# Gated DeltaNet chunk inverse: the last 64x64 merge level spread over both column halves of the TensorE array, with its evictions in two parts

## The chip, the cores and the metric

The kernel runs on one core of one Trainium2 chip. The metric is the device time of the whole launch in microseconds (us), as the median over runs of the same program. The profile is one profiled execution of the same program; its times are counted from the first instruction.

## The reference

One inference step of a two-layer decoder: layer 0 is a gated DeltaNet mixer, layer 1 an RWKV-7 mixer, each behind an RMSNorm and with a residual add. It runs on 1040 prompt tokens and on 8 x 8 sample tokens, 1104 columns in all, in fp32. What concerns the change is the chunk-wise delta rule of layer 0, which solves a unit lower triangular system for every chunk of 64 tokens and every head:

```python
L = jnp.where(strict, jnp.einsum('nbhik,nbhjk->nbhij', kb, k) * decay, 0.0)
A = L + jnp.eye(chunk, dtype=L.dtype)
rhs = jnp.concatenate([vb, kb * jnp.exp(gc)[..., None]], -1)
sol = lax.linalg.triangular_solve(A, rhs, left_side=True, lower=True, unit_diagonal=True)
u, wk = sol[..., :DV], sol[..., DV:]
...
v_new = u_c - jnp.einsum('bhck,bhkv->bhcv', w_c, S)
o = jnp.einsum('bhck,bhkv->bhcv', qd_c, S) + jnp.einsum('bhij,bhjv->bhiv', a_c, v_new)
S = S * jnp.exp(gl_c)[..., None, None] + jnp.einsum('bhck,bhcv->bhkv', kd_c, v_new)
```

There are 16 value heads and 8 key heads of width 128.

## The kernel before

Tokens are the columns of all activations, in three segments of 384, 384 and 336 columns (`SEGS`). Layer 0 loops over 8 key heads `j`; each carries two value heads. The kernel works with blocks of 128 tokens, so one segment of one key head has 6 systems (3 blocks x 2 value heads), and one key head has 18. The inverse of each 128x128 system is built in levels.

1. `gdn_prep` forms the scaled lower triangles `E` (kept as `G.LT`, one tile of 6 systems per segment) and sends their 32x32 diagonal blocks by DMA to a tile `invA` with one block per partition.
2. `inverse32` inverts these blocks on VectorE (31 steps of two instructions, L452 and L454).
3. The results come back by DMA into two tiles: `TT` (the transposed inverse, `TTs[...]`, one per segment) and `T1n`.
4. A first merge level joins 32x32 blocks to 64x64 ones. For each segment it forms Y (six systems, two halves, 32x32 matmuls into a PSUM bank of tag "r", evicted by VectorE at L668) and then U (evicted with a sign change by ScalarE through the helper at L62 into `TT`, and by VectorE at L679 into `T1n`).
5. A second merge level joins the 64x64 blocks to 128x128. This is the level that is changed. For each of the three segments there are six matmuls for Y: weights are rows 0 to 63 of `LT`, the moving data are rows 0 to 63 of `T1n`, and the output is partitions 64 to 127 of an "r" bank. One VectorE copy of 64x384 elements (L684) brings them into `Ys`, which lies in the tile that held `invA`. Then follow, for each segment, six matmuls for U: rows 64 to 127 of `Ys` and of `TT`, with the output on partitions 0 to 63 of an "r" bank, and one ScalarE activation of 64x384 elements (helper line L62, scale -1) into `TT`.

Where a matmul's operands start in the partitions sets the rows of the 128x128 array that it uses, and where its output starts sets the columns: all Y matmuls of this level use rows 0 to 63 and columns 64 to 127, all U matmuls rows 64 to 127 and columns 0 to 63.

After the inverse, `gdn_recur` steps through the 9 blocks of the head. In each step the state S is multiplied by the keys (`rA<-S,K`), VectorE forms X (L765), TensorE multiplies by `TT` (`rA<-X,TT`), ScalarE scales to w, TensorE forms the outputs and the state update, and VectorE updates S (L779). Its matmuls go to "r" banks as well; there are three of these.

All matmuls pass through the helper `mm` (L76), transposes through L73. The profile records each fp32 matmul as two passes, each with a weight load (PEld) and a matmul (PE).

The order of instructions on each engine is chosen by the framework's scheduler over layer 0 and the first part of layer 1, from the dependencies and its own timing model. It mixes the dense projections (`conv_tile` and `gdn_gate`: tiles dq, dk, dv, dz) of one head with the inverse and the recurrence of another. The last part, the RWKV wave, has its TensorE order written out by hand.

Of the kernel before, what the change touches and what calls it, by code (L numbers as in the profile page):

```python
# [10 lines left out]
AF = mybir.ActivationFunctionType  # L11
# [24 lines left out]
class Builder:  # L36
# [564 lines left out]
    def gdn_prep(self, j, G):  # L601
        nc, t, gp, fp = self.nc, self.t, self.gp, self.fp
# [7 lines left out]
        for s in range(3):  # L610
            q3 = slice(3 * s, 3 * s + 3)
            p = self.ps("f", 2, "sc")
# [37 lines left out]
        T1 = self.T1n  # L650
# [9 lines left out]
        v = lambda p, k: p[:, 0:6 * k].rearrange("p (c i) -> p c i", i=k)  # L660
        Y = [buf[:, 384 * s:384 * s + 384].rearrange("p (c i) -> p c i", i=64) for s in range(3)]
        for s, (LT, Ys) in enumerate(zip(G.LT, Y)):
            p = self.ps("r", 3, "Y")
# [5 lines left out]
        for s, (TT, Ys) in enumerate(zip(G.TT, Y)):  # L669
            p = self.ps("r", 3, "U")  # L670
# [8 lines left out]
            nc.vector.tensor_scalar(T1[32:64, 6 * s:6 * s + 6, 0:32], v(p, 32)[32:64], -1.0, None, op0=ALU.mult)  # L679
        for s, (LT, Ys) in enumerate(zip(G.LT, Y)):  # L680
            p = self.ps("r", 3, "Y")
            for c in range(6):
                self.mm(v(p, 64)[64:128, c], LT[0:64, c, 64:128], T1[0:64, 6 * s + c])
            nc.vector.tensor_copy(Ys[64:128], v(p, 64)[64:128])  # L684
        for s, (TT, Ys) in enumerate(zip(G.TT, Y)):
            p = self.ps("r", 3, "U")
            for c in range(6):
                self.mm(v(p, 64)[0:64, c], Ys[64:128, c], TT[64:128, c, 64:128])
            self.act(TT[0:64, :, 64:128], v(p, 64)[0:64], AF.Identity, scale=-1.0)

    def gdn_values(self, j, G, xh, xl):

# [1222 lines left out]
```

## Time and profile before

| | |
|---|---|
| median of 3 runs | 2376.5 us (2376.37 to 2380.79) |
| profiled execution, first to last instruction | 2369.3 us; no other time is given for it |
| TensorE matmul busy | 2188.7 us, 92% |
| TensorE weight load busy | 1982.0 us, 84% |
| VectorE busy | 1612.1 us, 68% |
| ScalarE busy | 1283.7 us, 54% |
| GpSimd busy | 1097.0 us, 46% |
| 64x64 matmul passes of this level, Y and U | 288 in 21.0 us and 288 in 19.5 us busy |
| Y evictions, 64x384 on VectorE | 24 in 13.2 us |
| U evictions, 64x384 on ScalarE | 24 in 11.1 us |

A busy time is the union of the instructions' durations on one engine, so passes that overlap count once; the mean of one instruction stands beside it in the groups' rows. Matmuls are pipelined, and the step from one start to the next is shorter than the duration of one.

### The profile page before, as it was taken

The numbers are of one execution on the slowest core, as the hardware profiler recorded it, in microseconds if no ns is written. First come the engines' busy times: TensorE is split into PE (matmuls) and PEld (weight loads), VectorE is DVE, ScalarE is ACT, GpSimd is POOL, SyncE is SP. The second block draws the span as 40 slices with busy tenths as digits, with TensorE's granted clock in tenths as the row PEclk, the third lists the DMA queues.
The fourth block names the chain that finished last, engine by engine and source line by source line (L and its number), as shares of the span: only waits on it lengthen the run. The fifth ranks groups of instructions, "written<-read, shape, count | busy, mean of one in ns | idle before, by whom it ended". The sixth has DMA issues, their size and how long they took to land. (4 is left out here: it accounts for less than half of the span.)

```text
span 2369.3 us, 54804 instructions
## 1 busy us (share of the span) xinstructions
PE 2188.7 (92%) x19737; PEld 1982.0 (84%) x19737; DVE 1612.1 (68%) x4201; ACT 1283.7 (54%) x3665; POOL 1097.0 (46%) x1542
## 2 busy tenths in 40 slices
PE   6989999999999999999999999998899899999896
PEld 5888989889898989898989998987778777778785
DVE  6878677685858686774346824479786567778754
ACT  5455645555656555466343746556454455667662
POOL 3435333443435343434232623444344667778764
PEclk9999999999999999999999999999999889999998
DMA  3323332323233333335162245566754544565543
GB/s 113 104 75 107 87 100 76 96 74 102 80 100 91 84 107 88 108 95 179 50 169 83 59 164 171 148 156 178 190 129 135 175 113 138 159 187 182 178 145 121
DMA packets 470922, 290.04 MB, mean 122 GB/s; under 512 B 188505, under 2 KB 456026, under 8 KB 470650
## 3 DMA queue, kind: packets, MB, share of 16 engines
q1 hardware_dynamic: 470650, 286.53, 42.8%
q8 instruction: 156, 2.56, 0.5%
q14 instruction: 116, 0.95, 0.1%
HBM read 200.53 MB, written 85.89 MB: 121 GB/s over the span
## 5 line engine op out<-in xcount | busy, mean ns | idle before, releaser
L90 POOL TENSOR_TENSOR wlo<-wraw,whi 128x512 fp32r<-128x512 f32 (+2 forms) x252 | 331.6, 1319 | 345.2 <-ACT whi L86 321.4
L76 PE MATMUL d<-xc,whi 128*128 128x384 f32 (+2 forms) x910 | 259.1, 341 | 5.3 <-POOL xc L90 2.5
L86 ACT CAST whi<-wraw 128x512 fp32r<-128x512 f32 (+2 forms) x252 | 151.5, 603 | 134.0 <-PE dq L76 50.4
L419 DVE SCALAR_TENSOR_TENSOR cvy<-raw,cw,cvy 128x408 f32<-128x408 f32 (+2 forms) x288 | 178.9, 634 | 17.0 <-ACT cvy L62 15.1
L76 PEld LDWEIGHTS d<-xc,whi 128*128 128x128 f32 (+1 forms) x910 | 167.6, 191 | 12.1 <-issue 3.4
L452 DVE TENSOR_TENSOR invtmp<-invA,invT 72x31 f32<-72x31 f32 (+31 forms) x403 | 165.5, 411 | 12.8 <-DMA invA<-ltd 4.4
L454 DVE TENSOR_TENSOR invT<-invT,invtmp 72x31 f32<-72x31 f32 (+31 forms) x403 | 165.5, 411 | 6.6
L76 PE MATMUL dz<-xc,whi 128*128 128x384 f32 (+1 forms) x480 | 149.6, 343 | 0.0
L76 PE MATMUL dv<-xc,whi 128*128 128x384 f32 (+1 forms) x480 | 146.8, 335 | 0.0
L76 PE MATMUL d<-xc,wlo 128*128 128x384 f32 (+2 forms) x428 | 142.4, 342 | 1.9 <-POOL wlo L90 1.9
L76 PE MATMUL d<-xa,whi 128*128 128x384 f32 (+3 forms) x450 | 139.7, 345 | 3.5 <-DVE xa L90 1.7
L868 POOL TENSOR_SCALAR Sb<-Sb,eglb 128x128 f32<-128x128 f32 x128 | 82.4, 662 | 87.8 <-DMA Sb<-in_state_gdn 62.3
L1506 POOL TENSOR_SCALAR y<-y,mv,grs 128x64 f32<-128x64 f32 x144 | 83.5, 600 | 41.3 <-DVE grs L106 39.6
L76 PE MATMUL dz<-xa,whi 128*128 128x384 f32 (+1 forms) x288 | 100.5, 349 | 0.0
L76 PE MATMUL dv<-xa,whi 128*128 128x384 f32 (+1 forms) x288 | 99.9, 347 | 0.1
L76 PEld LDWEIGHTS d<-xa,whi 128*128 128x128 f32 (+1 forms) x450 | 83.3, 190 | 11.0 <-issue 3.3
L76 PEld LDWEIGHTS dz<-xc,whi 128*128 128x128 f32 x480 | 89.9, 193 | 0.8
L76 PEld LDWEIGHTS dv<-xc,whi 128*128 128x128 f32 x480 | 88.6, 188 | 0.5 <-issue 0.4
L62 ACT ACTIVATE o<-rA,gcol 128x128 f32<-128x128 f32 x128 | 46.7, 372 | 72.4 <-DVE S L779 72.0
L76 PE MATMUL d<-xa,wlo 128*128 128x384 f32 (+3 forms) x252 | 85.9, 341 | 0.0
L76 PE MATMUL d<-xh,wlo 128*128 128x384 f32 (+1 forms) x256 | 83.8, 343 | 1.7 <-POOL wlo L90 1.7
L76 PEld LDWEIGHTS d<-xc,wlo 128*128 128x128 f32 (+1 forms) x428 | 81.1, 191 | 4.5 <-POOL wlo L90 2.2
(508 smaller groups left out, 7216.4 us busy)
## 6 DMA issues: line engine op xcount, KB each, us to landing
wraw<-in_gdn_w_in SPq DMA_DIRECT2D x96, 256.0 KB
wraw<-in_rwkv_w_rkvz SPq DMA_DIRECT2D x80, 256.0 KB
Sb<-in_state_gdn SPq DMA_DIRECT2D x64, 256.0 KB
wraw<-in_rwkv_w_o SPq DMA_DIRECT2D x40, 256.0 KB
E<-drow SPq DMA_DIRECT2D x24, 384.0 KB
attn<-drow SPq DMA_DIRECT2D x24, 384.0 KB
wraw<-in_gdn_w_out SPq DMA_DIRECT2D x36, 256.0 KB
out_s_gdn<-Sb SPq DMA_DIRECT2D x32, 256.0 KB
```

What stands on the lines that cost most here:

```text
L62: return self.nc.scalar.activation(out, in_, func, bias=bias, scale=scale, **kw)
L76: self.nc.tensor.matmul(out, lhsT, rhs, start=start, stop=stop)
L86: nc.scalar.copy(hi, x)
L90: e.tensor_tensor(lo, x, hi.bitcast(F32), op=ALU.subtract)
L419: nc.vector.scalar_tensor_tensor(y[:, 0:wd], raw[:, k:k + wd], cw[k], y[:, 0:wd], op0=ALU.mult, op1=ALU.add)
L452: nc.vector.tensor_tensor(tmp, A[:, j, j + 1:32].unsqueeze(2).broadcast_to([nb, n, m]), Tv[:, j, 0:m].unsqueeze(1).broadcast_to([nb, n, m] ...
L454: nc.vector.tensor_tensor(Tv[:, j + 1:32, 0:m], Tv[:, j + 1:32, 0:m], tmp, op=ALU.subtract)
L868: nc.gpsimd.tensor_scalar(Sb[:, u], Sb[:, u], self.eglb[:, hv, 4 * g + u:4 * g + u + 1], None, op0=ALU.mult)
L1506: nc.gpsimd.tensor_scalar(y6[:, q], y6[:, q], mv[:, q, 0:1], rs[:, q:q + 1], op0=ALU.subtract, op1=ALU.mult)
```

## The change

The six systems of a segment are dealt out to the two column halves: for Y, even systems stay in columns 64 to 127 and odd ones go to columns 0 to 63; for U the other way round. The rows of the array remain the same for both. In PSUM the six 64x64 results now lie in three 64-column slots on both partition halves, instead of six slots on one half. Each eviction is divided into two, one for each partition half: 64x192 elements each, written to every second system of the destination. Nothing else is edited; the number of matmuls is the same.

```diff
         for s, (LT, Ys) in enumerate(zip(G.LT, Y)):
             p = self.ps("r", 3, "Y")
+            w = p[:, 0:192].rearrange("p (c i) -> p c i", i=64)
             for c in range(6):
-                self.mm(v(p, 64)[64:128, c], LT[0:64, c, 64:128], T1[0:64, 6 * s + c])
-            nc.vector.tensor_copy(Ys[64:128], v(p, 64)[64:128])
+                a = 0 if c % 2 else 64
+                self.mm(w[a:a + 64, c // 2], LT[0:64, c, 64:128], T1[0:64, 6 * s + c])
+            for a, x in ((64, 0), (0, 1)):
+                nc.vector.tensor_copy(Ys[64:128, x::2], w[a:a + 64])
         for s, (TT, Ys) in enumerate(zip(G.TT, Y)):
             p = self.ps("r", 3, "U")
+            w = p[:, 0:192].rearrange("p (c i) -> p c i", i=64)
             for c in range(6):
-                self.mm(v(p, 64)[0:64, c], Ys[64:128, c], TT[64:128, c, 64:128])
-            self.act(TT[0:64, :, 64:128], v(p, 64)[0:64], AF.Identity, scale=-1.0)
+                a = 64 if c % 2 else 0
+                self.mm(w[a:a + 64, c // 2], Ys[64:128, c], TT[64:128, c, 64:128])
+            for a, x in ((0, 0), (64, 1)):
+                self.act(TT[0:64, x::2, 64:128], w[a:a + 64], AF.Identity, scale=-1.0)
```

## The prediction

> **What bounds the kernel now.** I read the page's busy shares and 40 slices first, then the windows of about one head each, then who waits for whom on TensorE, and last the matmuls of the edited step in order of time.
>
> ```profile
> span 2369.3 us, 54804 instructions
> ...
> PE 2188.7 (92%) x19737; PEld 1982.0 (84%) x19737; DVE 1612.1 (68%) x4201; ACT 1283.7 (54%) x3665; POOL 1097.0 (46%) x1542
> ...
> PE   6989999999999999999999999998899899999896
> ```
>
> TensorE is the full engine nearly everywhere. The windows sharpen this for the DeltaNet heads, which take about 130 us each (columns: stretch, length, then busy time of PE, PEld, DVE, ACT, POOL):
>
> ```profile
> core 0: us, PE busy (x) PEld busy (x) DVE busy (x) ACT busy (x) POOL busy (x), PEclk, DMA share, GB/s
> ...
> 230.00:360.00 130.00, 125.06 (x1025) 114.59 (x1026) 95.86 (x281) 71.93 (x231) 52.92 (x85) 0.98 0.33 89
> 360.00:490.00 130.00, 125.68 (x1030) 115.07 (x1029) 95.28 (x281) 72.56 (x231) 53.99 (x82) 0.98 0.34 92
> 490.00:620.00 130.00, 123.98 (x1017) 113.43 (x1018) 92.96 (x276) 71.12 (x229) 51.65 (x80) 0.99 0.33 90
> 620.00:750.00 130.00, 125.76 (x1044) 115.11 (x1043) 97.73 (x291) 74.17 (x238) 55.83 (x87) 1.00 0.35 94
> 750.00:880.00 130.00, 124.92 (x1025) 114.11 (x1025) 94.88 (x279) 71.75 (x230) 52.56 (x81) 0.99 0.32 89
> 880.00:1010.00 130.00, 126.56 (x1040) 116.55 (x1040) 95.85 (x288) 73.98 (x236) 55.94 (x85) 0.99 0.35 95
> ```
>
> PE is busy 125.3 of 130 us on average (96%), VectorE about 95, ScalarE about 73, and the granted clock is 0.98 to 1.00. So in these heads TensorE time is the time of the kernel, and the other two engines have 35 and 57 us of slack per head. What idles TensorE in the heads (window 140 to 1180 us) is small, and it is the recurrence, not the inverse:
>
> ```profile
> PE rA L76 <- DVE S L779: 8.7, 15, 2.1
> PE fhist L73 <- DVE lasts L437: 8.2, 7, 1.7
> PE rA L76 <- DVE X L765: 4.7, 7, 1.2
> ```
>
> **The change on TensorE.** The edited step is 48 groups of six 64x64 matmuls (8 heads, three segments, Y and U). Each fp32 matmul is recorded as two passes, so a group is 12 passes; all twelve sit in one quarter of the array now. The timeline of head 0 shows groups standing alone, two together and three together:
>
> ```profile
> 160.20 0.91 PE L76 MATMUL rY<-T1n,E 64*64 64x64 f32 x12
> ...
> 161.41 1.61 PE L76 MATMUL rY<-T1n,E 64*64 64x64 f32 x24
> ...
> 166.78 2.31 PE L76 MATMUL rU<-TT,invA 64*64 64x64 f32 x36
> ```
>
> Twelve more passes take 0.70 us more each time, so a pass follows the last one after 58 ns. One pass lasts 221 ns (rows below), so a lone group takes 0.91 - 0.22 = 0.69 us from its first start to its last: ten gaps of 58 ns and a first one of 0.11.
>
> After the change a group's even and odd matmuls alternate between the two column halves, over the same 64 rows. What matters is whether two column tiles that share their rows run side by side. Two places of this trace do that already. The state read (fsr) streams through four 32-column tiles on all 128 rows; and in the 32x32 level of this inverse the products marked invA,TT share rows 32 to 63 with half of those marked TT,invA, in the neighbouring 32 columns:
>
> ```profile
> 114.75 1.28 PE L76 MATMUL fsr<-Sb,kqm 128*32 128x128 f32 x34
> ...
> 155.97 0.19 PE L76 MATMUL rU<-invA,TT 32*32 32x32 f32 x1
> 155.98 0.21 PE L76 MATMUL rU<-TT,invA 32*32 32x32 f32 x2
> 156.00 0.19 PE L76 MATMUL rU<-invA,TT 32*32 32x32 f32 x1
> ...
> 172.27 0.38 PE L76 MATMUL rA<-X,TT 128*128 128x128 f32 x2
> ```
>
> ```profile
> L76 PE MATMUL rA<-X,TT 128*128 128x128 f32 x288 | 57.7, 287 | 4.8 <-DVE X L765 4.7
> L76 PE MATMUL fsr<-Sb,kqm 128*32 128x128 f32 x512 | 28.0, 280 | 0.9 <-POOL kqm L840 0.6
> L76 PE MATMUL rY<-T1n,E 64*64 64x64 f32 x288 | 21.0, 221 | 0.0
> L76 PE MATMUL rU<-TT,invA 64*64 64x64 f32 x288 | 19.5, 220 | 0.1
> ```
>
> Two rA passes over the full array are 0.38 - 0.29 = 0.09 us apart. The fsr passes stream the same 128 columns, yet 33 starts fit into 1.28 - 0.28 = 1.00 us: 30 ns each, about a third. In the 32x32 level a whole round of three tiles takes 0.03 us. So shared rows do not serialise.
>
> The Trainium skill, TensorE: Matmul & The Clock Gate, section Part 3 (Packing small matmuls), says that a weight load overlaps matmuls in flight only where the row group differs; here the row group is the same, and by that rule the change would gain nothing. The fsr rows speak against it, and I keep it as a rival.
>
> New group: each half has six passes, 0.11 + 4 x 0.058 = 0.34 us from first start to last, and the second half starts about 0.01 us after the first, so 0.35 instead of 0.69. Where groups stand together, 0.70 per group becomes 0.35. Saving 0.34 x 48 = 16.3 us. Something of this exists already: where a U follows a Y without a gap, as in four of the eight heads (the first is shown), the last three Y passes run beside U passes:
>
> ```profile
> 283.14 0.73 PE L76 MATMUL rY<-T1n,E 64*64 64x64 f32 x9
> 283.66 0.27 PE L76 MATMUL rU<-TT,invA 64*64 64x64 f32 x1
> 283.71 0.22 PE L76 MATMUL rY<-T1n,E 64*64 64x64 f32 x1
> 283.76 0.22 PE L76 MATMUL rU<-TT,invA 64*64 64x64 f32 x1
> ...
> 283.88 1.39 PE L76 MATMUL rU<-TT,invA 64*64 64x64 f32 x21
> ```
>
> That is 3 x 0.055 us in four heads, 0.7 us that is not saved a second time: 15.6 us. The halves alternate one by one in all 48 groups of the changed kernel's instruction order, so the scheduler does not undo it. I let 96% (the heads' busy share) reach the end: 15.0 us.
>
> **The change on the evictions.** Each group's one eviction becomes two of half the columns, 24 more on VectorE (Y, L684) and 24 more on ScalarE (U, through L62). No row is 64x192; these are around it:
>
> ```profile
> L668 DVE COPY invA<-rY 32x192 f32<-32x192 f32 x48 | 17.1, 357 | 6.8 <-PE rY L76 5.9
> L684 DVE COPY invA<-rY 64x384 f32<-64x384 f32 x24 | 13.2, 560 | 7.7 <-PE rY L76 7.3
> L784 DVE COPY o<-rA 64x128 f32<-64x128 f32 x16 | 4.7, 295 | 0.2
> L62 ACT ACTIVATE TT<-rU 32x192 f32<-32x192 f32 x48 | 15.4, 321 | 23.5 <-PE rU L76 22.9
> L62 ACT ACTIVATE TT<-rU 64x384 f32<-64x384 f32 x24 | 11.1, 477 | 1.2 <-PE rU L76 1.2
> L62 ACT ACTIVATE UV<-rA 64x128 f32<-64x128 f32 x144 | 35.8, 273 | 50.6 <-PE rA L80 50.3
> L76 PEld LDWEIGHTS rU<-TT,invA 64*64 64x64 f32 x288 | 17.7, 135 | 1.4 <-issue 1.1 <-DVE invA L684 0.2
> ```
>
> The same 192 elements per partition cost 357 ns on VectorE and 321 ns on ScalarE; the 64x128 rows (295 and 273) bound it below, the undivided evictions (560 and 477) above. I take 357 and 321: 2 x 357 - 560 = 154 ns more per Y and 2 x 321 - 477 = 165 ns more per U, hence 0.46 + 0.50 = 0.96 us per head, 7.7 us over the kernel if nothing hid it. What hides it is the dense projection work that stands between Y and U on TensorE: the last row shows 0.2 us in total for which a U waited on a Y copy. In the new order 4 of 8 heads keep 10 or more matmuls between the last Y and the first U and one keeps 7; the other three have none or two, but there the first Y stands well before the last, or the later U groups stand 10 or more matmuls on. I charge 1.0 us for two or three half-microsecond waits where this cover is thin; the ends are 0 and 7.7. The second copy waits only for the odd half, which ends with the even one, so the queue behind it (conv taps and the recurrence's X and S on VectorE) is late by 0.15 us, no more. The three "r" banks come free as much later. No DMA is added or moved by the text of the change.
>
> **The schedule.** The scheduler places instructions anew: the two TensorE orders agree up to head 0's merge and over the last 3,636 matmuls (the hand-ordered wave), and differ by local swaps between. That has no sign that I can derive. Its size I estimate from the six like windows: their busy times scatter by 0.88 us (standard deviation), so a redraw of some 12 windows (148 to 1,810 us) moves the sum by 0.88 x sqrt(12) x sqrt(2) = 4.3 us, or 5.5 us 8 times in 10.
>
> **Sum.** 15.0 - 1.0 = 14.0 us. The page gives the profiled execution as its span, 2369.3 us, and no other time; the median of the runs is 2376.5, 7.2 more. So the span should become 2355 and the time 2376.5 - 14.0 = 2362.5, with 2357 to 2368 as this case's own range.
>
> **Rivals.**
> *The evictions come onto the path* (0.15). U waits for the second Y copy and the recurrence for the second U eviction, in every head: all 7.7 us are paid, 15.0 - 7.7 = 7.3 remains, 2369. For it: the chain Y, copy, U, eviction is serial, and three heads have little between Y and U. Against it: the 0.2 us row, and VectorE's 35 us of slack. The Trainium skill, TensorEngine Tiling (Array Packing), section PSUM Bottleneck, warns of just this, that eviction may take over once tiling speeds up the matmuls.
> *The recurrence's waits grow* (0.13), the case on the slower side. Removing TensorE work and swapping neighbours leaves less filler between a head's S, X and w steps. The price is the 8.7 us in 15 waits, 0.58 each. It cancels the 14.0 at 24 more such waits and is slower by 0.2% (4.8 us) from 33, four per head; then about 2381. Typical of this case is 20 to 30 more, 2374 to 2380. Against it: only 15 such waits stand in 1040 us, and the work removed is 2 us in 130.
> *Shared rows serialise* (0.06), so that the change does not do what it says. If the halves simply take turns, nothing is saved and 1.0 is paid: 2377. If every change of half waits as a first pass does, 0.11 us a gap, a group takes 11 x 0.11 = 1.2 us instead of 0.69, 0.5 x 48 = 24 us more: 2401. The fsr rows are against both. The skill's row-group rule, above, belongs here.
>
> **How the numbers follow.** The forecast has 0.66. The range 2355 to 2374 takes the forecast with its schedule scatter, the eviction case and the lower edge of the waits case. A measurement can tell about 0.2%, 4.8 us: faster is below 2371.7, the same is up to 2381.3. Faster: 0.64 of the forecast, 0.12 of the evictions, 0.01 of the waits: 0.77. Slower: 0.05 of the waits, 0.03 of the serialising rows and 0.02 for schedule scatter on top: 0.10. The same: 0.13.
>
> **What would show it.** In the new profile, a lone group of twelve 64x64 passes at 0.57 us instead of 0.91, and the busy time of the rY and rU 64x64 matmuls down from 21.0 and 19.5 us to about 13 and 12; evictions of 64x192 near 357 and 321 ns, 48 of each; waits of rU on the L684 copies (then L687) below 2 us in total. The forecast is wrong if the twelve still take 0.9 us, if TensorE's waits on S, X and w grow by more than 5 us, or if a stretch after 1180 us, where nothing was edited, grows by several.

## The result and the profile after

The changed kernel takes 2390.7 us (median of 9 runs, 2380.6 to 2401.1) against 2375.4 for the one before on the same chip: a ratio of 1.0065, 95% interval 1.0046 to 1.0084. Forecast were 2362.5 us and a gain of 14.0; it became about 15 us slower, outside the range. Ratios and intervals, here and below, leave out the one slow run of all, 2407.5 us in experiment e8. The profiled execution spans 2386.5 us, 17.2 more than before's. The lines of its page that answer to those shown of before, with the granted TensorE clock by slices (PEclk, in tenths of full speed):

```profile
span 2386.5 us, 54833 instructions
...
PE 2186.4 (92%) x19737; PEld 1978.4 (83%) x19737; DVE 1627.2 (68%) x4225; ACT 1294.1 (54%) x3689; POOL 1101.1 (46%) x1542
...
PE   6989999999999999999999999988989888899995
...
PEclk9999999999999999999999999999999899999998
```

The groups of the edited step, from the views by form of TensorE, VectorE and ScalarE (busy time and mean, then idle time before them):

```profile
L76 PE MATMUL rU<-TT,invA 64*64 64x64 f32 x288 | 13.9, 250 | 0.5 <-PE rU L76 0.4
L76 PE MATMUL rY<-T1n,E 64*64 64x64 f32 x288 | 13.7, 243 | 4.7 <-DVE T1n L679 4.6
...
L687 DVE COPY invA<-rY 64x192 f32<-64x192 f32 x48 | 17.1, 356 | 5.4 <-PE rY L76 4.5
...
L62 ACT ACTIVATE TT<-rU 64x192 f32<-64x192 f32 x48 | 15.6, 325 | 2.9 <-PE rU L76 2.3
```

The edited matmuls fell from 21.0 + 19.5 = 40.5 us busy to 27.6, with means of 243 and 250 ns that a lower clock in some of them has lengthened; the divided evictions take 356 and 325 ns. The evictions are as forecast, the matmuls nearly so (about 25 us was forecast; see e9). But TensorE's whole busy time fell by 2.3 us only, and its waits in the window from 140 to 1180 us have another make-up than before:

```profile
PE fhist L73 <- DVE lasts L437: 10.0, 7, 2.0
PE rA L76 <- DVE S L785: 6.3, 12, 1.4
PE rA L76 <- ACT w L62: 4.9, 4, 2.8
PE rY L76 <- DMA T1n<-g_t: 4.9, 3, 3.9
PE rY L76 <- DVE T1n L679: 4.6, 5, 2.2
PE dk L76 <- DVE zg L726: 4.1, 3, 1.7
```

Two rows of before that the prediction does not show:

```profile
PE rY L76 <- DMA T1n<-g_t: 3.9, 1, 3.9
PE rA L76 <- ACT w L62: 3.2, 6, 0.9
```

Not there before are Y's waits on VectorE's T1n (4.6 us, up to 2.2) and those of the projection dk on `zg`, the output gate (4.1). The first is clear in head 2. ScalarE and VectorE in the timeline, with TensorE's passes:

```profile
421.76 0.56 PE L76 MATMUL rY<-T1n,E 64*64 64x64 f32 x12 [2.20 <-DVE T1n L679]
422.83 0.90 PE L76 MATMUL rY<-T1n,E 64*64 64x64 f32 x12 [0.51 <-DVE T1n L679]
...
420.25 0.49 ACT L62 ACTIVATE zg<-dz 128x384 f32<-128x384 f32 x1 [4.41 <-DMA ogd<-zg]
420.64 1.31 ACT L62 ACTIVATE TT<-rU 32x192 f32<-32x192 f32 x4
...
420.77 0.55 DVE L726 SCALAR_TENSOR_TENSOR zg<-zg,dz 128x384 f32<-128x384 f32 x1 [4.55 <-ACT zg L62]
421.36 0.35 DVE L679 TENSOR_SCALAR T1n<-rU 32x192 f32<-32x192 f32 x1
```

The scheduler has put `zg<-dz` ahead of the TT evictions of the first merge level on ScalarE, and ScalarE stands idle 4.41 us for a transfer. VectorE's product of zg waits 4.55 us for that, T1n is queued behind the product, and TensorE stands still for 2.20 and 0.51 us. The first lone group of this head takes 0.56 us. The second of the two waiting groups takes 0.90 us again, because the clock has just fallen (columns: stretch, length, busy times, then PEclk, DMA share, GB/s):

```profile
416.00:422.00 6.00, 3.80 (x68) 3.20 (x62) 1.39 (x4) 1.68 (x6) 0.00 (x0) 1.00 0.28 73
422.00:433.00 11.00, 10.49 (x83) 9.12 (x80) 4.26 (x10) 6.52 (x20) 5.82 (x9) 0.53 0.56 172
```

From 422.6 to 432.9 us TensorE is granted half its clock (0.5; called half clock from here on). The same stands behind the merges of heads 1 and 3 in this execution, 10.2 us each.

### The profile page after: what moved, and what is told of

It is laid out like the page before. It is cut to its first block, busy times and chain, and to the rows that moved or that the text cites. A ratio compares the mean times of both kernels' runs of the same rounds, so it can differ in the third digit from the quotient of the medians.

```text
span 2386.5 us, 54833 instructions
## 1 busy us (share of the span) xinstructions
PE 2186.4 (92%) x19737; PEld 1978.4 (83%) x19737; DVE 1627.2 (68%) x4225; ACT 1294.1 (54%) x3689; POOL 1101.1 (46%) x1542
## 5 line engine op out<-in xcount | busy, mean ns | idle before, releaser
L419 DVE SCALAR_TENSOR_TENSOR cvy<-raw,cw,cvy 128x384 f32<-128x384 f32 (+2 forms) x288 | 181.6, 643 | 22.0 <-ACT cvy L62 20.6
L76 PE MATMUL d<-xh,whi 128*128 128x384 f32 (+1 forms) x256 | 82.7, 338 | 3.7 <-ACT xh L86 2.7
```

What stands on the lines that cost most here:

```text
L76: self.nc.tensor.matmul(out, lhsT, rhs, start=start, stop=stop)
L419: nc.vector.scalar_tensor_tensor(y[:, 0:wd], raw[:, k:k + wd], cw[k], y[:, 0:wd], op0=ALU.mult, op1=ALU.add)
```

## The experiments

The questions were three: is the time in the code (matmuls in both halves, divided evictions) or in the order of the instructions; does the placement save what was forecast; and if not all, where does it go. To hold the order fixed, some kernels carry a list of the order for every engine, added after the program is built; each instruction gets an order edge to the one before it on its own engine, which makes no engine wait for another:

```diff
-        Builder(tc, ins, outs).build()
+        x = Builder(tc, ins, outs)
+        x.extra = {}
+        x.build()
+        _pin(nc, tc, x.extra)
...
+        for a, b in zip(out, out[1:]):
+            tc.add_manual_dep(b, a.name, dep, reason="pin")
```

A second half of an eviction goes directly behind its first half. Line numbers in these kernels are 24 or 25 higher, in e4 as in the change. No run pins before's code to before's own order and changes nothing else; e3 (1.0012) and e10 (0.9996) come nearest to showing that the pinning itself costs nothing that can be measured. All results, each against the kernel before run on the same chip:

| run | code | order | median us (runs) | ratio, 95% interval |
|---|---|---|---|---|
| the change | new | new | 2390.7 (9) | 1.0065, 1.0046 to 1.0084 |
| e1 | new | of before | 2364.4 (12) | 0.9975, 0.9953 to 0.9997 |
| e2 | of before | new | 2385.2 (12) | 1.0054, 1.0028 to 1.0080 |
| e3 | evictions divided only | of before | 2373.3 (12) | 1.0012, 0.9990 to 1.0035 |
| e4 | Y only | its own | 2404.5 (6) | 1.0140, 1.0099 to 1.0180 |
| e5, as e1 | new | of before | 2368.3 (12) | 0.9984, 0.9959 to 1.0010 |
| e6 | new | of before, TT earlier | 2364.4 (12) | 0.9974, 0.9956 to 0.9993 |
| e7 | new | new, TT and T1n earlier | 2386.7 (12) | 1.0052, 1.0032 to 1.0072 |
| e8 | of before, Y copies lengthened | of before | 2384.5 (10) | 1.0050, 1.0024 to 1.0076 |
| e9 | new | of before, three waits mended | 2364.6 (12) | 0.9955, 0.9938 to 0.9971 |
| e10 | of before | as e9 | 2373.0 (12) | 0.9996, 0.9976 to 1.0015 |

**e1 and e5: the changed code in the order of before.**

> The changed matmuls and evictions, with every engine's instructions pinned to the order of the kernel before (each second eviction directly behind its twin). Theory A (the new instruction order is what costs; the placement in two column halves saves what the prediction said): 12 to 16 us faster than before, about 2361, granted clock 0.97 or above, and no half-clock stretch of 10 us in heads 1 to 3. Theory B (the placement itself costs: small matmuls packed into half the time, or the divided evictions, pull the clock down or stall): as slow as the changed kernel, about 2390, with half-clock stretches after the merges. Theory C (gain and loss are both small and the difference is scatter between runs): between 2370 and 2385.

> The changed code in the order of the kernel before, as in the run of that name, once more on the same chip as the next three. Expected: 0.9975 of before again (0.995 to 1.000), and in the heads 1, 3 and 5 again a TensorE wait of about 0.7 us between the first and the second U group and a half-clock stretch of 3.4 us right behind it.

Two sets of 12 runs, 0.9975 and 0.9984: 4 to 6 us faster than before (e5 by itself is not told apart from it), and about 20 us faster than the same code in the new order. So the new order, not the edit, makes the change slow. But the gain is a third of the forecast, and less than the 12 us that e1 was expected to show at least. Where it goes is seen in head 1, in e1's timeline and its windows:

```profile
284.87 0.56 PE L101 MATMUL rY<-T1n,E 64*64 64x64 f32 x12 [0.34 <-DVE T1n L704]
...
286.91 0.56 PE L101 MATMUL rU<-TT,invA 64*64 64x64 f32 x12 [0.76 <-PE rU L101]
...
289.56 0.91 PE L101 MATMUL rU<-TT,invA 64*64 64x64 f32 x12
```

```profile
284.00:287.50 3.50, 2.25 (x41) 1.72 (x39) 2.97 (x8) 2.23 (x7) 1.39 (x2) 1.00 0.64 234
287.50:291.00 3.50, 3.50 (x23) 3.02 (x23) 0.47 (x2) 3.44 (x12) 2.98 (x6) 0.56 0.37 109
```

TensorE now comes to the third Y and the second U before their operands are there, waits 0.34 and 0.76 us where before has no such wait, and then runs 3.4 us at half clock, in which the last group takes 0.91 us as if nothing had been moved. Half clock stands behind the merges of heads 1, 3 and 5 in e1. In e5, the same program, it was expected there again, and it came in head 5 alone. In head 0 the saved time is lost one step on, in the recurrence's first step. Before, and then e5 (TensorE and ScalarE):

```profile
174.17 0.49 PE L76 MATMUL rA<-w,attn 128*128 128x128 f32 x2 [0.94 <-ACT w L62]
```

```profile
176.27 0.80 PE L101 MATMUL rA<-w,attn 128*128 128x128 f32 x2 [3.06 <-ACT w L87]
...
169.29 1.28 ACT L87 ACTIVATE E<-E,gcol 128x128 f32<-128x128 f32 x4 [0.52 <-POOL E L604]
170.47 0.64 ACT L87 ACTIVATE TT<-rU 64x192 f32<-64x192 f32 x2
```

U is done at 167.7 us, but its eviction on ScalarE is queued behind activations of E (exponentials of the decays, here called scalings) that wait for GpSimd, which waits for a transfer. The about 2 us that TensorE saved became 2.1 us more of waiting (3.06 instead of 0.94). The divided evictions have a part in it: from GpSimd's first step on E to w it is 9.85 us in e1, e5 and e6, and 8.94 before.

Summed over the heads, from the first Y of head 0 to the last `rA<-S,K` of head 7, the records of TensorE and of its clock give this, one execution each (idle: neither matmul nor weight load; the last column is the length less the idle time and half the half-clock time):

| kernel | length us | idle | at half clock | work at full clock |
|---|---|---|---|---|
| before | 1015.5 | 38.2 | 23.9 | 965.4 |
| e10 | 1016.2 | 37.6 | 27.3 | 964.9 |
| e3 | 1017.2 | 37.5 | 30.6 | 964.5 |
| e8 | 1022.9 | 39.7 | 34.1 | 966.1 |
| e1 | 1013.1 | 43.9 | 37.5 | 950.4 |
| e5 | 1010.4 | 43.7 | 33.0 | 950.3 |
| e6 | 1009.7 | 42.6 | 34.1 | 950.1 |
| e9 | 1008.4 | 43.5 | 30.7 | 949.5 |

Before's execution has a granted clock of 0.973, high among the 35 runs of before beside e5 (0.964 to 0.974, 0.969 on average), so its half clock is on the low side. The work is 15.0 to 15.9 us less with the new matmuls, as forecast, in all four. In e5, 5.5 us of it went back into idle time and 9.1 / 2 = 4.5 into half clock, and 5.1 remained.

**e2: the code of before in the new order.**

> The matmuls and evictions of the kernel before, with every engine pinned to the order that the changed kernel had. Theory A (the order costs): slower than the changed kernel by the saved matmul time, 2395 to 2405, with the half-clock stretches of 10 us after the merges of heads 1 to 3. Theory B (the placement costs): as before, about 2375. Theory C: between 2370 and 2385.

1.0054, nearly all of the change's 1.0065, with no edited instruction in it. Together with e1 and e5 this makes the square of code and order: the order costs about 13 us with the old code and some 20 with the new, and the placement saves 4 to 6 us in the old order and nothing that can be measured in the new one. The 2395 to 2405 us that were expected of e2 for this case did not come: they count the whole matmul saving, which in the new order is not seen. On average the cost of the order is not half clock: the granted clock is 0.9690 over e2's 12 runs and 0.9692 over the 29 of before beside them.

**e3: only the evictions divided.** The matmuls stay in one half.

```diff
-            nc.vector.tensor_copy(Ys[64:128], v(p, 64)[64:128])
+            q = [nc.vector.tensor_copy(Ys[64:128, x::2], v(p, 64)[64:128, x::2]) for x in (0, 1)]
+            self.extra[q[0].ins.name] = q[1].ins.name
```

and likewise for U.

> Only the evictions are divided (every second system each), the matmuls stay in one column half, and every engine is pinned to the order before. This prices the divided evictions alone. Theory A: 0 to 4 us slower than before. If the divided evictions lie on the path (the prediction's rival): about 8 us slower. Theory B with the evictions as the cause: 15 us or more slower.

1.0012, which is 2.9 us with an interval of -2.4 to 8.3: not told apart from nothing, nor by the times alone from all of the 7.7 us. The trace speaks for nothing: the idle time of the heads is 37.5 us against 38.2 and their work at full clock 964.5 against 965.4. But these evictions are cheaper than those of the change, as their rows show:

```profile
L709 DVE COPY invA<-rY 64x192 f32<-64x192 f32 x48 | 14.8, 358 | 6.9 <-PE rY L101 6.7
...
L87 ACT ACTIVATE TT<-rU 64x192 f32<-64x192 f32 x48 | 12.4, 317 | 1.2 <-PE rU L101 1.2
```

Here both halves read the same PSUM partitions, and the second one starts before the first has ended: 48 x 358 ns are 17.2 us, but VectorE is busy 14.8. In the change the halves lie on different partitions, and they do not overlap (17.1 and 15.6 us). So e3 adds 1.6 + 1.3 = 2.9 us of eviction time to before, and the change 3.9 + 4.5 = 8.4. What the change's own evictions cost at the end was not measured.

**e4: only Y in both halves, scheduler free.**

> Only Y is dealt out to both column halves, with its evictions divided; U as before; the scheduler orders freely and gives a third order. Matmul saving half of the whole, about 8 us. Theory A: anything between 8 us faster and 15 us slower, decided by the half-clock time in the heads, and not halfway between before and after. Theory B: halfway, about 2383.

1.0140, the slowest of all and about 33 us over before, with half of the change; at most 15 were expected. The scheduler's third order cost more than the change itself. The profiled execution is the fastest of the six runs, 19 us below their median; its heads take 1040.0 us, 51.0 of it idle and 47.8 at half clock. The granted clock of the six runs is 0.9615 on average, against 0.9692 for before.

**e6: e1 with one group of TT evictions earlier.** In heads 1, 3, 5 and 7 ScalarE's evictions of the third 32x32 U come ahead of five `attn` scalings that wait for GpSimd (`attn` holds the decayed scores).

> The changed code in the order of the kernel before, with one thing moved: in heads 1, 3, 5 and 7 ScalarE evicts the third 32x32 U group directly behind the second, instead of behind five activations of attn that wait for GpSimd. That releases the last T1n, the last Y and the U groups earlier. Theory A1 (the rest of the matmul saving is lost because TensorE now reaches the Y-copy-U chain of these heads too early, waits, and the clock falls to half): the waits before the last Y and between the U groups go, most of the half-clock stretches of heads 1, 3 and 5 go with them, and the time falls by a further 4 to 8 us, to about 0.994 of before. Theory A2 (the rest is lost elsewhere, or in scatter): no difference from the same code without the move.

0.9974, no different from e1 and e5; the expected gain did not come. The trace tells why: the wait on T1n is gone, and the next one stands. Head 1 on TensorE and VectorE:

```profile
287.49 0.56 PE L101 MATMUL rU<-TT,invA 64*64 64x64 f32 x12 [0.57 <-PE rU L101]
...
286.10 0.56 DVE L751 SCALAR_TENSOR_TENSOR zg<-zg,dz 128x384 f32<-128x384 f32 x1 [1.94 <-ACT zg L87]
286.66 1.48 DVE L711 COPY invA<-rY 64x192 f32<-64x192 f32 x4
```

The wait is put down to "PE rU", but what comes last is VectorE's copy of the second Y: its matmuls ended before 285, and the copies start at 286.66 because VectorE stands at `zg` for 1.94 us first.

**e7: the new order with two such places mended.** In heads 2 and 3 the TT evictions and the T1n forms come ahead of zg.

> The changed code in the changed kernel's own order, with one thing moved in heads 2 and 3: the second and third 32x32 U groups are evicted (ScalarE, and VectorE into T1n) before the gate activation zg that waits for a DMA, instead of behind it. Theory A: these two heads' waits of 2.2 and 1.0 us before Y and their half-clock stretches of 10.2 us each go, so about 3 + 2 x 10.2 / 2 = 13 us at most and 6 to 13 us in all, which brings it from 1.0065 to 1.001 to 1.004 of before. If the cost of the order is spread over many small waits: less than 3 us.

1.0052: 3 us by the ratios came back, within their intervals nothing. The wait of 2.20 us in head 2 is gone, and in head 3 that of 1.01. But the idle time of the heads is 53.8 us where the change has 48.8; waits of U on a transfer (5.2 us in 7, where the change has 2.7) and others took their place. The time at half clock in the heads did fall, to 37.5 us from the change's 54.6. The two long waits that could be seen, and the half clock behind them, were not what the order costs.

**e8: the old code made late.** In heads 1, 3 and 5 the first copy of Y is made four times, 1.7 us more of VectorE in each; nothing else differs from before.

```diff
-            nc.vector.tensor_copy(Ys[64:128], v(p, 64)[64:128])
+            q = [nc.vector.tensor_copy(Ys[64:128], v(p, 64)[64:128]) for _ in range(4 if s == 0 and j in (1, 3, 5) else 1)]
...
```

> The kernel before in its own order; in heads 1, 3 and 5 the first Y copy of the 64x64 level is made four times instead of once (1.7 us more on VectorE, the same values), so that TensorE waits between Y and U. If a wait of this length between small matmuls is enough to pull the clock down, the profile shows a half-clock stretch of 3.4 us or more behind each of the three merges, where the kernel before has none, and the time rises by more than the waits themselves: 3 x 1.2 us of waiting and 3 x 1.7 us of half clock, about 9 us. If the packing of the matmuls is what pulls it down, no such stretch and at most 4 us more.

12 us (1.0050, interval 1.0024 to 1.0076) for three delays of 1.7 us, on an engine that is busy 68%. In head 1 (TensorE, VectorE, and the clock after it):

```profile
287.08 0.88 PE L101 MATMUL rU<-TT,invA 64*64 64x64 f32 x12 [0.83 <-PE rY L101]
288.21 1.34 PE L101 MATMUL rU<-TT,invA 64*64 64x64 f32 x12 [0.25 <-DVE invA L709]
...
284.63 2.35 DVE L709 COPY invA<-rY 64x384 f32<-64x384 f32 x4
```

```profile
288.00:291.50 3.50, 3.29 (x19) 3.17 (x20) 0.63 (x2) 1.84 (x5) 2.28 (x5) 0.57 0.51 149
```

TensorE waits 0.83 and 0.25 us and then has half its clock for 3.4 us; before has neither there. In head 5 the clock falls too; in head 3 TensorE waits as well (0.74 and 0.25 us), but the clock stays up, although a fall was expected behind each of the three. So a small lateness in the chain from T1n over Y to U is enough for waits, and a fall of the clock can stand behind them, with the old matmuls too. The profiled execution shows 7.4 us of the 12 in the heads, 5.1 as half of 10.2 us more of half clock. Over the runs, the granted clock is 0.966 on average against 0.969 for before; as span times lost clock, that is up to 8 of the 12 us.

**e9 and e10: the waits mended.** The order of before with e6's move; VectorE's copies of the second Y ahead of `zg` in heads 1, 3, 5, 7; the TT evictions of head 0 ahead of the last scalings of E. e9 has the new code, e10 that of before.

> The changed code in the order of before, with three groups of evictions issued earlier: as in e6 ScalarE's third group of 32x32 TT evictions before the five attn scalings in heads 1, 3, 5, 7; in the same heads VectorE's second copies of Y before the zg product that waits for ScalarE; and in head 0 the three TT evictions of U before the last four E scalings. In e5 and e6 TensorE stands 2.0 to 2.1 us longer than in before ahead of the second group of U (sum of the odd heads) and 2.1 us longer ahead of the first rA of w and attn in head 0; these two waits should go. Theory W (what the placement frees turns into waits of TensorE behind ScalarE and VectorE, each of which can be taken away): idle time of the heads falls from 42.6 us (e6) to about 39, and the time to about 0.994 to 0.996 of before, 2358 to 2364 us where before has 2373. Rival X (the waits only move to the next place, or the time goes into half-clock stretches whatever the waits are): the named waits go, the idle time of the heads or the half-clock time grows elsewhere, and the ratio stays at 0.997 to 0.998.

> The code of before (no column halves, undivided evictions) in exactly the order of e9. Theory W: these evictions were not what before's TensorE waited for (before has 0.1 us ahead of the second group of U), so the order by itself is worth 0 to 2 us: ratio 0.999 to 1.001, and e9 stands 10 us or more below this one. Rival Y (the new place of these evictions is simply a better order, whatever the matmuls do): this kernel falls by as much as e9 does against e1, 4 us or more, to 0.998 or below.

e9 is at 0.9955, e10 at 0.9996, on the same chip: in one order, the placement is worth 0.41% or 9.7 us between these ratios (4 to 16 us by both intervals together). The order alone is worth nothing, so this is not just a better order. e9 beats both kernels, by 10.7 us (0.45%) and by about 1.1%. Against e1, e5 and e6 (0.9975, 0.9984, 0.9974) the step to 0.9955 is not clear of the intervals. And the idle time of the heads, which was to fall from 42.6 us to about 39, is 43.5, as one rival had it: mended waits came back elsewhere. What e9 mended and what not:

```profile
286.61 0.74 PE L101 MATMUL rU<-TT,invA 64*64 64x64 f32 x19
...
173.92 0.49 PE L101 MATMUL rA<-w,attn 128*128 128x128 f32 x2 [3.10 <-ACT w L87]
...
798.75 0.56 PE L101 MATMUL rU<-TT,invA 64*64 64x64 f32 x12 [1.32 <-issue]
...
1051.01 0.56 PE L101 MATMUL rY<-T1n,E 64*64 64x64 f32 x12 [1.22 <-DVE T1n L704]
...
168.84 3.60 ACT L87 ACTIVATE E<-E,gcol 128x128 f32<-128x128 f32 x12
172.35 1.12 ACT L111 CAST whi<-wraw 128x512 fp32r<-128x512 f32 x2
```

In head 1 the last Y and two groups of U run as one without a wait, and the clock stays up. In head 0 the mend failed: the wait of 3.10 us is as long as it was, since w itself is queued on ScalarE behind the twelve scalings and two weight casts. In head 5 a wait of 1.32 us stands, and in head 7 one of 1.22 came up. With the 2.2 us by which head 0's wait exceeds that of before, these make 4.7 us; added to the 9.7 gained they come near the 14.0 of the forecast. That sum mixes one execution with medians, and these three waits were not mended; so it is an estimate.

## Why the prediction was wrong

**The matmul step was right.** A lone group takes 0.56 us (forecast 0.57). In e9, with hardly any half clock in these groups, the two busy times are 12.7 and 11.0 us, 16.8 less than before (forecast 16.3), and the work at full clock is 15 to 16 us less (forecast 15.6):

```profile
L101 PE MATMUL rY<-T1n,E 64*64 64x64 f32 x288 | 12.7, 225 | 1.2 <-DVE T1n L704 1.2
...
L101 PE MATMUL rU<-TT,invA 64*64 64x64 f32 x288 | 11.0, 222 | 1.3 <-issue 1.3
```

Three groups of U together take 1.26 us instead of 2.31. Two column halves over the same rows run side by side, so the rival of serialising rows falls. With it falls, for this case, what the prediction drew from the row-group rule of the Trainium skill (TensorE: Matmul & The Clock Gate, section Part 3 (Packing small matmuls)): by it nothing was to be gained, and the three groups of U together ran in about half the time.

**The evictions' size was right, their charge is not settled.** They take 356 and 325 ns (forecast 357 and 321). e3 was to price them, and measures 2.9 us (-2.4 to 8.3) at the end, but with only 2.9 of the change's 8.4 us of added eviction time. In head 0 they lie on the path: the chain from E to w, for which TensorE waits, is 9.85 us in e1, e5 and e6, 9.09 in e3 and 8.94 before. That is 0.9 us in one head, nearly the 1.0 us that was charged for all. That all 7.7 us are paid was not tested by itself.

**The step "96% reaches the end" failed.** It took the share of time in which TensorE is busy for the share of a saving that counts. In the order of before only 4 to 6 of 15 us reached the end (e1, e5). The serial chain through ScalarE and VectorE (TT, T1n, Y, its copy, U) goes on at its own pace. The 0.2 us row of U's waits was read as cover, but a row of waits does not tell how long an operand had been ready. Before's timelines do: in 19 of the 24 groups of U the copy of Y had ended 1.0 to 4.6 us before the group began, in the other five, all in heads 1, 3 and 5, only 0.06 to 0.79 us. Two microseconds less per head on TensorE, and there the evictions come last. One more reading was off: of the waits shown as the recurrence's, the 8.2 us of fhist belong to the projections' convolution, and the inverse's largest wait, Y's 3.9 us on T1n's transfer, is not among them.

**The schedule step failed most.** It was called a scatter without a sign, 4.3 us by standard deviation. It cost about 13 us by e2 and some 20 by e1 and e5 against the change. Both orders that the scheduler made anew for a local edit, that of the change (with either code) and that of e4, were slower than before's (1.0054, 1.0065, 1.0140). The estimate came from the busy times of six windows of one order, which hold how far its parts differ, not how one order differs from another, so the sum put the order at nothing without a ground for it. That the new order puts `zg` ahead of the TT evictions, on an engine that then stands for a transfer, could be read in the changed kernel's instruction order; it was called local swaps.

**The waits rival was right in sign and wrong in place.** The waits on S, X and w, 8.7 + 4.7 + 3.2 us before, are 6.3 + 2.6 + 4.9 after. What grew were waits ahead of the merge itself (T1n 4.6 us, none before), on zg (4.1) and on fhist (1.8 more). The half clock, of which the prediction has no term, is 54.6 us in the heads of the one profiled execution, against 23.9; but e2, whose heads also have 54.6, has on average over its runs the clock of before.

**Open.** Which swaps of the new order cost the 13 us is not settled: e7 took away the long waits on T1n in heads 2 and 3 and got some 3 us back. Of the 17.2 us in the profiled execution, only 4.6 lie in the heads (1020.1 us against 1015.5) and 10.2 in the hand-ordered wave, whose TensorE order is that of before (530.1 us against 519.9, with 69.4 us at half clock against 55.1). The prediction had named such growth after 1180 us as a sign against it. The six runs with both Y and U in two halves idle 68.8 to 71.0 us there, the other six 64.7 to 66.3; no run explains this. And half-clock stretches differ between executions of one kernel: e1 and e5, the same program, show 64.8 and 94.4 us of them from the first Y to the wave.

## What to carry to other kernels

A local edit under a scheduler is two changes, the instructions and the order: pin the order to that of before, measure the edit in it, and measure the new order with the old code. Time taken from a full engine counts only as far as the operands of its next steps are already there; read how long each had been ready, and try to move up the evictions that will come last along with the edit. Here the kernel with both was the fastest (0.9955, against 0.9996 for the moves without the edit and 0.9974 to 0.9984 for the edit in before's order with none or one of them), though only the first of these differences is clear of the intervals.

## What the runs showed of the hardware

Falls of TensorE's clock stand behind waits far below 3 us. Behind merges with waits of 0.34 and 0.76 us (e1), 0.83 and 0.25 (e8), or 2.20 and 0.51 (the change), it fell to half for 3.4 us or 10.2. The Trainium skill, TensorE: Matmul & The Clock Gate, section A second HAM failure mode: psum-queue depth-cycling, tells of the clock swinging when TensorE is often idle for a little between groups of matmuls. The traces agree that such a swing exists. The same page's rule in the section HAM oscillation, against idle gaps of more than about 3.4 us, would miss these places, since no wait in them is that long.

Why like waits sometimes bring a fall and sometimes not can be read from the twelve traces. In each of them the clock changes only on a grid of 3.41 us (to within 5 ns), and the idle time that falls into one window of that grid goes with what follows. Counted are the windows at full clock from 140 to 1180 us, idle as in the table of the heads:

| idle in the window | windows | followed by half clock |
|---|---|---|
| under 0.9 us | 3297 | 3 |
| 0.9 to 1.3 us | 99 | 9 |
| 1.3 us and more | 142 | 90 |

Of the 12 falls under 1.3 us, 11 stand behind matmuls of a merge. In head 1 of e1 and of e8 the two waits fall into one window (1.16 and 1.05 us idle), and the clock falls behind it. In head 3 of e8 they fall into two (0.71 and 0.25), and it stays up. This is a pattern over traces; no run sets the idle time of a window by itself.

Lateness cost more than its length: 5.1 us of VectorE work in e8 cost 12 us (interval 6 to 18).

Two eviction pieces of 64x192 that read the same 64 PSUM partitions start 0.28 us apart on VectorE and 0.21 on ScalarE (e3, before the first has ended); from different partition halves it is 0.37 and 0.32 to 0.34 us (the change), one after the other. Why is not shown.
